# Sliding-window attention block: a new slot table for a block's small tasks, and the norm factors ahead in their slots

## The chip, the cores and the metric

One NeuronCore of a Trainium2 chip runs the whole kernel. The metric is the device time of one execution in microseconds. TensorE is PE in the profile, VectorE is DVE, ScalarE is ACT, GpSimd is POOL, and SyncE, whose queue issues the transfers spoken of here, is SP.

## The reference, cut to what matters

One layer of the trunk is computed: RMSNorm, a sliding-window grouped-query attention with sinks and a SiLU gate, the residual and a final RMSNorm, on 4096 rows of 1024 columns.

```python
xn = rms_norm(x, norm_g[0])
q, k, v, z = jnp.split(xn @ w_in, [1024, 1280, 1536], axis=-1)     # 16 heads, 4 k/v heads of 64
o = banded_attention(q_heads(q), kv_heads(k), kv_heads(v), t5_table, 128, sinks)
y = (merge_heads(o) * jax.nn.silu(z)) @ w_out
return rms_norm(x + y, final_g)
```

## The kernel before, in words

The rows are worked in 16 blocks (`tb`) of 256 rows, each as two tiles of 128. A number is held as a high and a low half in 16 bits, and a product of two such numbers is three passes on PE. The three large projections (q, z and the output o) multiply their operands as 2 x 2 blocks by a scheme of seven products with sums of blocks (`11`, `s1`, `s2`, `12`, `s3`, `s4`, `22` on the left, `11`, `t1`, `t2`, `21`, `t3`, `22`, `t4` on the right) in place of eight plain ones; the first two or three blocks still use the plain form, since the summed weights are only made then. A product of q or z (`product_t`, L324) is 48 matmuls, one of o (`product_o`, L610) 12. The weights of z and o come from DRAM again for each block, 1 MB for a product, by `load_s` (L303) into the tile `ws` of three buffers; in the trace the sources are named wzss, wzs, wost and wos, and wqs for the seventh of q.

A block's work is cut into small tasks, and a table (`STEADY`) gives each task a slot. A slot is about one product on PE; 25 slots make a block, and a block's tasks spread over 62 slots, so that two to three blocks are under way at once. Slots named here count from 0 to 24 within a block's stretch: slot 36 of a table is slot 11 of the next block's stretch. Within a slot the tasks are emitted by phase, in the order bank (copying a finished product out of its bank), attn, sum, split, soft, load, main (the product) and scores. Up to slot 104 a scheduler orders the engines' work; from slot 105 on (block 4, from about 425 us) PE, DVE, ACT and POOL keep exactly the order of emission, and each engine waits in place for what its next instruction needs.

The tasks that matter below:

- `x_square`, `x_factor`, `x_row`, `x_scale`, `x_split` prepare the next block's x. ACT squares (L238), DVE and POOL make the factor 1/rms of each row in `power` (ms L242, rr L244), PE turns two columns of factors into a row (`x_row`, L257, in slot 13), DVE multiplies.
- `out_square`, `out_factor`, `out_store` are the final norm of a tile of 128 output rows: ACT squares (L630), `power` again, DVE multiplies (L637) and SP stores (L639).
- `load_r` (L587) loads the residual of the next output into the one tile `r`, which also holds the output until it is stored. So its transfer waits in SP's queue until the second store has landed, and what stands behind it in the queue waits too.
- A `Pair` (two groups of heads by one tile of rows) goes through scores (L491), post (DVE, L509 and L518), exps (ACT, L526), normalise (DVE, ACT), turn (transposes on PE, L545; pt and pm, L547 to L551), values (L569) and gate (L576). The tile `c` of a pair has two buffers for four pairs a block.
- `proj_k` (L343), `proj_v` (L393), `evac_k` (L377 to L387), `done_q` (L371, L372).

Of the kernel before, what the change touches and what calls it, by code (L numbers as in the profile page):

```python
# [58 lines left out]
def tile_swa_block(ctx, tc, x, xt, t5, norm_g, final_g, w_q, w_kv, w_z, sinks, w_out, hot, out):  # L59
# [589 lines left out]
    def at(phase, s, f, *a):  # L649
        work_of[s][phase].append(lambda: f(*a))  # L650
# [53 lines left out]
    def plain_t(slots, tb, key, names, left, place, done):  # L704
# [8 lines left out]
        "o": (43, 44, 46, 48, 49, 47, 52),  # L713
        "qplain": (0, 1, 2, 3, 4, 5, 6, 6), "zplain": (11, 13, 14, 15, 16, 17, 20, 20),
        "oplain": (43, 44, 46, 47, 48, 49, 50, 50),
# [6 lines left out]

        "pairs": {(0, 0): (10, 11, 14, 15, 20, 13, 14, 16, 20, 22, 25, 28),
# [6 lines left out]
    }  # L730
    SHORT = (0, 1, 2, 3, 5, 2, 3, 4, 5, 7, 8, 9)

    def moved(pairs, by):
# [3 lines left out]
                 zplain=(11, 12, 13, 14, 15, 16, 17, 17), xload=8, pairs=moved(STEADY["pairs"], (7, 5, 4, 2)))  # L737
    LAST = dict(STEADY, vd=13, dv=15, zs12=18, zp22=19, zs22=20,
                pairs={p: tuple(s + d for d in SHORT) for p, s in zip(STEADY["pairs"], (11, 14, 17, 20))},
                o=(31, 32, 33, 35, 36, 34, 37), op=(34, 35, 35, 37), on=(37, 38), om=(37, 38), os=(38, 39), res=32,  # L740
                ysum={"s1": 30, "s2": 31, "s4": 32, "s3": 33},
                ysplit={"11": 29, "s1": 30, "12": 31, "s2": 31, "s4": 32, "s3": 34, "22": 34})

# [2 lines left out]
    def block(tb):  # L746
# [3 lines left out]
        def there(v):  # L750
            if isinstance(v, dict):
                return {k: there(a) for k, a in v.items()}
            return tuple(s0 + s for s in v) if isinstance(v, tuple) else s0 + v

        S = {k: there(v) for k, v in plan.items()}
# [60 lines left out]
        at("load", S["res"], load_r, tb)  # L816
        for t in range(2):
            at("soft", S["on"][t], out_square, tb, t)
            at("soft", S["om"][t], out_factor, tb, t)
            at("split", S["os"][t], out_store, tb, t)  # L820
        if tb + 1 < NTB:
            at("load", S["xload"], load_xin, tb + 1)
            at("load", S["xload"], load_xf, tb + 1)
            for t in range(2):
                at("soft", S["xq"][t], x_square, tb + 1, t)
            at("soft", S["xm"], x_factor, tb + 1)
            at("attn", S["xr"], x_row, tb + 1)
            for i in range(2):
                at("split", S["xscale"][i], x_scale, tb + 1, i)
                at("split", S["xsplit"][i], x_split, tb + 1, i)  # L830
            if tb + 1 >= min(PLAIN["q"], PLAIN["z"]):
                for n in SUM:
                    at("sum", S["xsum"][n], x_sum, tb + 1, n)
                    at("split", S["xsumsplit"][n], x_sum_split, tb + 1, n)

    for tb in range(NTB):
        block(tb)
# [84 lines left out]
```

## Time and profile before

| | us |
|---|---|
| median of three runs | 1491.39 (1479.51 to 1492.14) |
| the profiled execution, its own time | 1487.63 |
| its span, first to last instruction | 1485.9 |
| PE busy | 1371.5 (92%) |
| DVE busy | 1147.8 (77%) |
| ACT busy | 877.5 (59%) |
| POOL busy | 409.3 (28%) |

The span and what lies around it (1.7 us) make the profiled execution's own time. PE is the busiest engine; the other 114 us are the stretches in which no matmul runs. The mean granted TensorE clock is 0.979 of full speed.

### The profile page before, as it was taken

The numbers are of one execution on the slowest core, as the hardware profiler recorded it, in microseconds if no ns is written. First come the engines' busy times: TensorE is split into PE (matmuls) and PEld (weight loads), VectorE is DVE, ScalarE is ACT, GpSimd is POOL, SyncE is SP. The second block draws the span as 40 slices with busy tenths as digits, with TensorE's granted clock in tenths as the row PEclk, the third lists the DMA queues.
The fourth block names the chain that finished last, engine by engine and source line by source line (L and its number), as shares of the span: only waits on it lengthen the run. The fifth ranks groups of instructions, "written<-read, shape, count | busy, mean of one in ns | idle before, by whom it ended". The sixth has DMA issues, their size and how long they took to land.

```text
span 1485.9 us, 39435 instructions
## 1 busy us (share of the span) xinstructions
PE 1371.5 (92%) x16234; PEld 1097.1 (74%) x16234; DVE 1147.8 (77%) x2847; ACT 877.5 (59%) x2313; POOL 409.3 (28%) x402
## 2 busy tenths in 40 slices
PE   5998998998989999898998989999998999999986
PEld 4897687686776878777686777878777686877842
DVE  7489867689577877787777878787787788788883
ACT  8467756576455656565565655556565565656662
POOL 1003422344223231331313223141322323232133
PEclk9999999999999999999999999999999999999998
DMA  9975765968866483765738567493855748374665
GB/s 369 274 274 171 279 244 188 344 245 319 309 230 256 155 322 138 277 232 194 303 103 313 196 218 276 146 354 116 301 210 215 258 165 325 141 266 181 215 239 227
DMA packets 70660, 356.22 MB, mean 240 GB/s; under 512 B 8752, under 2 KB 10832, under 8 KB 40656
## 3 DMA queue, kind: packets, MB, share of 16 engines
q1 hardware_dynamic: 61952, 336.92, 62.2%
q10 hardware_dynamic: 8528, 16.78, 3.0%
q8 instruction: 127, 2.08, 0.6%
q14 instruction: 53, 0.43, 0.1%
HBM read 318.03 MB, written 35.65 MB: 238 GB/s over the span
## 4 chain that ended last, share of the span: by engine, by line
PE 52%; DVE 18%; DMA 17%; ACT 9%; issue 3%; POOL 1%; SPq 1%; ACTq 0%; POOLq 0%; DVEq 0%
PE pa L324 12%; PE pb L324 10%; PE pc L610 8%; DMA ws<-wzss 5%; PE pa L610 4%; PE o L569 4%; PE s L491 3%; DVE q L372 3%; PE pc L324 3%; DMA out<-r 3%; PE pb L610 3%; DVE pm L551 2%; PE tp L545 2%; DVE pt L548 2%; DVE wsp L136 2%
## 5 line engine op out<-in xcount | busy, mean ns | idle before, releaser
L324 PEld LDWEIGHTS <-ws 128*128 128x128 f16 x6192 | 368.1, 101 | 40.8 <-DMA ws<-wzss 21.4
L324 PEld LDWEIGHTS <-wq 128*128 128x128 f16 x4800 | 274.1, 98 | 21.6 <-issue 14.8
L610 PEld LDWEIGHTS <-yo 128*128 128x128 f16 x1380 | 133.8, 99 | 162.9 <-issue 15.8
L526 ACT ACTIVATE c<-c,m 128x129 f32<-128x129 f32 x512 | 198.8, 392 | 21.9 <-DVE m L518 21.5
L610 PE MATMUL pc<-ws,yo 128*128 128x512 f16 x768 | 181.1, 386 | 6.1 <-DMA ws<-wost 3.2
L518 DVE CUSTOM_DVE_ANT_0 c<-s,bias,sink 128x128 f32<-128x128 f32 x496 | 153.6, 348 | 38.3 <-PE tp L545 31.5
L535 ACT ACTIVATE c<-c,rl 128x128 f32<-128x128 f32 x256 | 86.5, 394 | 149.3 <-DVE rl L531 146.1
L244 POOL TENSOR_TENSOR rr<-ms,mhalf 128x1 f32<-128x1 f32 x64 | 35.8, 566 | 416.5 <-DVE ms L242 372.0
L548 DVE SCALAR_TENSOR_TENSOR pt<-tp,pt 128x512 f16<-128x512 f32 x128 | 87.7, 688 | 47.9 <-ACT pt L547 46.7
L491 PE MATMUL s<-K,q 128*128 128x192 f16 x1024 | 109.7, 247 | 12.1 <-DVE m L518 9.6
L597 POOL TENSOR_TENSOR y<-y,y 128x512 f32<-128x512 f32 x52 | 78.3, 1506 | 142.0 <-DVE y L576 80.9
L324 PE MATMUL pb<-xs,ws 128*128 128x128 f16 x1872 | 111.1, 219 | 4.3 <-DMA ws<-wzss 2.4
L537 DVE TENSOR_SCALAR c<-c,rl 128x128 f32<-128x128 f32 x256 | 109.0, 467 | 4.0
L625 POOL TENSOR_TENSOR r<-r,mc 128x512 f32<-128x512 f32 x52 | 74.8, 1443 | 127.2 <-ACT mc L353 73.0
L491 PEld LDWEIGHTS <-q 128*128 128x128 f16 x1024 | 84.9, 98 | 28.8 <-DVE m L518 13.4
L353 ACT ACTIVATE mc<-pa 128x512 f32<-128x512 f32 x68 | 40.5, 595 | 110.7 <-PE pa L324 100.4
L161 POOL TENSOR_TENSOR wst<-wst 128x512 f32<-128x512 f32 x48 | 67.0, 1406 | 111.1 <-ACT wst L196 39.1
L526 ACT ACTIVATION_READ_ACCUMULATOR c<-c,m 128x1 f32 x512 | 96.8, 189 | 0.0
L551 DVE TENSOR_TENSOR pm<-pt,own_m 128x1024 f16<-128x1024 f16 x128 | 92.3, 723 | 3.5
L509 DVE COPY_PREDICATED s<-sel,s 128x128 f32<-128x128 int32 x256 | 72.8, 289 | 25.9 <-PE s L491 25.5
L547 ACT ACTIVATE pt<-tp 128x512 f16<-128x512 f32 x128 | 72.7, 593 | 32.4 <-PE tp L545 28.6
L610 PE MATMUL pa<-ws,yo 128*128 128x512 f16 x384 | 88.3, 379 | 3.5 <-ACT yo L603 1.3
(124 smaller groups left out, 2688.0 us busy)
## 6 DMA issues: line engine op xcount, KB each, us to landing
ws<-wos SPq DMA_DIRECT2D x63, 1024.0 KB, 6.1
ws<-wzss SPq DMA_DIRECT2D x52, 1024.0 KB, 5.9
ws<-wost SPq DMA_DIRECT2D x52, 1024.0 KB, 5.6
ws<-wzs SPq DMA_DIRECT2D x47, 1024.0 KB, 5.2
xin<-in_x SPq DMA_DIRECT2D x32, 512.0 KB, 7.3
xf<-in_xt SPq DMA_DIRECT2D x32, 512.0 KB, 3.9
r<-in_x SPq DMA_DIRECT2D x32, 512.0 KB, 4.3
out<-r SPq DMA_DIRECT2D x32, 512.0 KB, 4.4
```

The lines of the kernel that those rows point to most:

```text
L324: nc.tensor.matmul(place(p, c), left(kc, wi)[:, c * P:(c + 1) * P], right_x(tb, right, kc, xi), start=fresh and c == 0 and k == 0, stop=c ...
L491: nc.tensor.matmul(s[:, hp, 0:3 * HD], lhs, rhs, start=hl == 0, stop=hl == 1)
L509: nc.vector.copy_predicated(dst, sel[:, None, :].to_broadcast([P, 2, HD]), src)
L518: nc.vector.tensor_tensor_reduce(out=cu, in0=sv, in1=b, scale=-1.0 / SCORE, scalar=sink[:, g, r, hp:hp + 1], op0=OP.add, op1=OP.min, accum ...
L526: nc.scalar.activation(cu, cu, AF.Exp, bias=self.m[:, u:u + 1], scale=-1.0, accum_out=self.l[:, u:u + 1])
L535: nc.scalar.activation(cu, cu, AF.Copy, scale=rl[:, u:u + 1])
L537: nc.vector.tensor_scalar(cu, cu, rl[:, u:u + 1], None, op0=OP.mult)
L548: nc.vector.scalar_tensor_tensor(w[:, 1], p, SP, w[:, 0], op0=OP.mult, op1=OP.subtract)
L551: nc.vector.tensor_tensor(self.pm[e].rearrange("p l (h q) -> p (l h) q", h=4), w.rearrange("p l (h q) -> p (l h) q", h=4), own_m[:, None, ...
L597: nc.gpsimd.tensor_tensor(Y[(tb, *dst)], Y[(tb, *l)], Y[(tb, *r)], op=op)
L610: nc.tensor.matmul(p, YO[left][:, yi, c * P:(c + 1) * P], right(c, wi), start=fresh and k == 0, stop=k == 11, skip_group_check=not fresh)
L625: nc.gpsimd.tensor_tensor(r, r, m, op=OP.add)
```

## The change

Two phases change: `out_factor` and `x_factor` go from soft to attn, so that they are emitted ahead of the sum, split and soft tasks of their slot, behind the attn tasks that were registered earlier. And some 45 numbers of the slot table change. None of the products of q, k, v, z and o moves, and no instruction is added or taken away.

```diff
-        "qp22": 10, "qs11": 8, "qs12": 8, "qs22": 13, "vd": 15, "dv": 17,
-        "zp22": 20, "zs11": 18, "zs12": 26, "zs22": 22,
-        "op": (49, 48, 47, 56), "on": (50, 57), "om": (54, 59), "os": (56, 61), "res": 40,
+        "qp22": 9, "qs11": 7, "qs12": 6, "qs22": 15, "vd": 14, "dv": 18,
+        "zp22": 20, "zs11": 18, "zs12": 29, "zs22": 26,
+        "op": (50, 48, 49, 55), "on": (52, 56), "om": (54, 58), "os": (58, 61), "res": 40,
...
-        "pairs": {(0, 0): (10, 11, 14, 15, 20, 13, 14, 16, 20, 22, 25, 28),
+        "pairs": {(0, 0): (10, 11, 14, 20, 22, 12, 13, 17, 18, 20, 25, 27),
...
-        "xload": 5, "xq": (11, 11), "xm": 12, "xr": 13, "xscale": (14, 16), "xsplit": (15, 19),
+        "xload": 5, "xq": (11, 11), "xm": 12, "xr": 13, "xscale": (14, 14), "xsplit": (16, 19),
...
-            at("soft", S["om"][t], out_factor, tb, t)
+            at("attn", S["om"][t], out_factor, tb, t)
...
-            at("soft", S["xm"], x_factor, tb + 1)
+            at("attn", S["xm"], x_factor, tb + 1)
```

A pair's twelve numbers are the slots of scores, post, exps, normalise and turn of its first group, the same five of its second, then values and gate.

On PE, in slots 12 and 13 of a block that is emitted by hand, this stood before (L393 is the last matmul of `proj_v`, L257 is `x_row`, L324 the product `s1` of z):

```order
L393 LDWEIGHTS xb
L393 MATMUL pc<-wkv,xb 128x256
L257 MATMUL tp<-ident,rr 128x128 x2
L324 LDWEIGHTS ws
L324 MATMUL pa<-xs,ws 128x128
```

and this stands now:

```order
L491 LDWEIGHTS q
L491 MATMUL s<-K,q 128x192
L257 MATMUL tp<-ident,rr 128x128 x2
L324 LDWEIGHTS ws
L324 MATMUL pa<-xs,ws 128x128
```

The second scores of the first pair (eight matmuls, L491) have moved from behind product `s1` to ahead of `x_row`.

On DVE, slots 6 to 9, from the gate of a pair (L576) to the copy with which `evac_k` begins (L377), before:

```order
L576 SCALAR_TENSOR_TENSOR y_19519<-o,z 128x512
L637 SCALAR_TENSOR_TENSOR r<-r,rr,gf 128x1024
L548 SCALAR_TENSOR_TENSOR pt_19583<-tp,pt_19583 128x512
L551 TENSOR_TENSOR pm_19586<-pt_19583,own_m 128x1024
L548 SCALAR_TENSOR_TENSOR pt_19593<-tp,pt_19593 128x512
L551 TENSOR_TENSOR pm_19596<-pt_19593,own_m 128x1024
L372 SCALAR_TENSOR_TENSOR q<-cc,q 64x512 x4
L377 COPY K<-K 128x8x128
```

and now:

```order
L576 SCALAR_TENSOR_TENSOR y_19520<-o,z 128x512
L372 SCALAR_TENSOR_TENSOR q<-cc,q 64x512 x2
L548 SCALAR_TENSOR_TENSOR pt_19585<-tp,pt_19585 128x512
L551 TENSOR_TENSOR pm_19588<-pt_19585,own_m 128x1024
L372 SCALAR_TENSOR_TENSOR q<-cc,q 64x512 x2
L242 TENSOR_SCALAR ms<-ss 128x1
L548 SCALAR_TENSOR_TENSOR pt_19631<-tp,pt_19631 128x512
L551 TENSOR_TENSOR pm_19634<-pt_19631,own_m 128x1024
L637 SCALAR_TENSOR_TENSOR r<-r,rr,gf 128x1024
L377 COPY K<-K 128x8x128
```

The first store's multiplication (L637) has gone from ahead of the two turns to behind them, the splits of q (L372) from behind them to ahead and between, and the factor of the second store (L242), which stood behind `evac_k`, is ahead of it. From L377 to the factor of x (`ms<-rs`, L242, right behind the two turns of slot 12) the rows of DVE are otherwise the same in both kernels.

On SP, from the loads of the next x (L105) to the weights of `s4` of z, this stands now:

```order
L105 DMA xf<-in_xt 128x1024 x2
L639 DMA out<-r 128x1024
L303 DMA ws<-wzss_96 128x4096
L303 DMA ws<-wzs_93 128x4096
L99 DMA xin<-in_x 128x1024 x2
L639 DMA out<-r 128x1024
L587 DMA r<-in_x 128x1024 x2
L303 DMA ws<-wzss_92 128x4096
```

Nothing has moved there: the kernel before has the same transfers in the same order.

## Rows read from the trace of the kernel before

**Rows 1.** The page's first part, busy time of each engine, share of the span and instructions; then two stretches of the span, the scheduled part with block 4's beginning and the part in the order of emission, with the busy time of each engine, PE's granted clock, the share of the DMA engines and GB/s.

```profile
PE 1371.5 (92%) x16234; PEld 1097.1 (74%) x16234; DVE 1147.8 (77%) x2847; ACT 877.5 (59%) x2313; POOL 409.3 (28%) x402
...
0.00:425.00 425.00, 380.62 (x4652) 311.38 (x4652) 326.42 (x809) 269.91 (x648) 113.20 (x112) 0.98 0.75 270
425.00:1440.00 1015.00, 961.69 (x11456) 773.99 (x11458) 801.59 (x2010) 593.95 (x1641) 282.04 (x277) 0.98 0.63 228
```

**Rows 2.** The timeline of PE around slots 12 to 16 of block 12, and of the same place in block 7 (last row): start us, us, engine, line, operation, out<-in, form, count, idle before and who ended it.

```profile
1133.63 0.32 PE L257 MATMUL tp<-ident,rr 128*128 128x128 f32 x1 [2.42 <-POOL rr L244]
...
1134.30 2.84 PE L324 MATMUL pa<-xs,ws 128*128 128x128 f16 x48
1136.98 0.82 PE L491 MATMUL s<-K,q 128*128 128x192 f16 x8
...
1147.44 2.85 PE L324 MATMUL pa<-xb,ws 128*128 128x128 f16 x48 [2.75 <-DMA ws<-wzss]
...
708.16 4.48 PE L324 MATMUL pa<-xb,ws 128*128 128x128 f16 x48 [3.68 <-DMA ws<-wzss]
```

**Rows 3.** Seven stretches of 3 us, each right behind `x_row` of one block (7 to 12, and 6 first), columns as in rows 1; PE's granted clock stands behind the busy times.

```profile
606.80:609.80 3.00, 3.00 (x27) 2.94 (x28) 2.25 (x3) 0.00 (x0) 1.77 (x2) 0.50 0.88 315
694.00:697.00 3.00, 3.00 (x52) 2.99 (x53) 2.20 (x2) 0.02 (x1) 1.72 (x2) 1.00 0.87 337
784.30:787.30 3.00, 2.91 (x25) 2.62 (x25) 2.58 (x3) 0.00 (x0) 2.09 (x3) 0.50 0.93 351
873.00:876.00 3.00, 2.86 (x25) 2.63 (x25) 2.57 (x3) 0.00 (x0) 2.08 (x3) 0.50 0.89 335
961.80:964.80 3.00, 3.00 (x31) 3.00 (x29) 1.37 (x2) 0.00 (x0) 0.85 (x1) 0.50 0.59 240
1047.10:1050.10 3.00, 2.83 (x26) 2.67 (x26) 2.53 (x3) 0.00 (x0) 2.04 (x3) 0.50 0.90 333
1134.40:1137.40 3.00, 3.00 (x55) 3.00 (x54) 2.03 (x2) 0.22 (x1) 1.51 (x2) 1.00 0.81 315
```

**Rows 4.** The timeline ahead of `x_row` in block 9, all engines, columns as in rows 2.

```profile
868.68 1.08 ACT L547 ACTIVATE pt<-tp 128x512 f16<-128x512 f32 x2
...
869.30 0.69 DVE L548 SCALAR_TENSOR_TENSOR pt<-tp,pt 128x512 f16<-128x512 f32 x1 [0.43 <-ACT pt L547]
...
871.97 0.21 DVE L242 TENSOR_SCALAR ms<-rs 128x1 f32<-128x1 f32 x2
...
872.20 1.06 POOL L244 TENSOR_TENSOR rr<-ms,mhalf 128x1 f32<-128x1 f32 x2 [8.81 <-DVE ms L242]
```

**Rows 5.** SP's queue: the issue of the second store of each block (every other L639 row is left out), one row for a block.

```profile
602.58 0.38 SPq L639 DMA_DIRECT2D out<-r  x1
...
690.21 0.38 SPq L639 DMA_DIRECT2D out<-r  x1
...
780.41 0.38 SPq L639 DMA_DIRECT2D out<-r  x1
...
869.09 0.38 SPq L639 DMA_DIRECT2D out<-r  x1
...
956.67 0.40 SPq L639 DMA_DIRECT2D out<-r  x1
...
1043.15 0.39 SPq L639 DMA_DIRECT2D out<-r  x1
...
1129.93 0.38 SPq L639 DMA_DIRECT2D out<-r  x1
...
1218.71 0.39 SPq L639 DMA_DIRECT2D out<-r  x1
```

**Rows 6.** SP's queue around the second store of block 12 (its own row is in rows 5), the waits of that queue between 640 and 1240 us (who waited for whom, us in total, times, longest), and the queue at the next-to-last block, where no load of x stands ahead of the store.

```profile
1129.02 0.81 SPq L99 DMA_DIRECT2D xin<-in_x  x2
...
1138.82 0.80 SPq L587 DMA_DIRECT2D r<-in_x  x2
1139.68 2.69 SPq L303 DMA_DIRECT2D ws<-wzss  x2
...
SPq L587 <- DMA out<-r: 57.8, 7, 8.9
...
1306.02 0.34 SPq L639 DMA_DIRECT2D out<-r  x1
1310.29 0.81 SPq L587 DMA_DIRECT2D r<-in_x  x2
```

**Rows 7.** DVE's timeline in slots 7 to 11 of block 9: the first turn's pt, the four splits of q, the copy that begins `evac_k`, the second store's multiplication.

```profile
851.80 0.69 DVE L548 SCALAR_TENSOR_TENSOR pt<-tp,pt 128x512 f16<-128x512 f32 x1 [1.38 <-ACT pt L547]
...
854.58 2.81 DVE L372 SCALAR_TENSOR_TENSOR q<-cc,q 64x512 f16<-64x512 f32 x4
857.40 0.43 DVE L377 COPY K<-K 128x1024 f16<-128x1024 f16 x1
...
867.59 1.28 DVE L637 SCALAR_TENSOR_TENSOR r<-r,rr,gf 128x1024 f32<-128x1024 f32 x1
```

**Rows 8.** One row of the list of waits over the whole span: who waited for whom, us in total, times, longest.

```profile
DVE c L518 <- PE tp L545: 31.5, 11, 2.9
```

**Rows 9.** DVE's timeline at the kernel's end, the last two stores' multiplications.

```profile
1478.43 1.27 DVE L637 SCALAR_TENSOR_TENSOR r<-r,rr,gf 128x1024 f32<-128x1024 f32 x1
...
1480.59 1.28 DVE L637 SCALAR_TENSOR_TENSOR r<-r,rr,gf 128x1024 f32<-128x1024 f32 x1 [0.66 <-POOL rr L244]
```

More of the change, by code (lines that the diff above doesn't have):

```diff
@@ L739, in tile_swa_block @@
                 pairs={p: tuple(s + d for d in SHORT) for p, s in zip(STEADY["pairs"], (11, 14, 17, 20))},
-                o=(31, 32, 33, 35, 36, 34, 37), op=(34, 35, 35, 37), on=(37, 38), om=(37, 38), os=(38, 39), res=32,
+                o=(31, 32, 33, 35, 36, 34, 37), op=(34, 35, 35, 37), on=(37, 38), om=(38, 39), os=(38, 39), res=32,
                 ysum={"s1": 30, "s2": 31, "s4": 32, "s3": 33},
```

12 rows, old and new, of the table STEADY are left out of this document.

## The prediction

> **What bounds the kernel now.** I read the shares first: PE is busy for 92% of the span [rows 1], so the only time to be won is the 114 us in which it does nothing, and what a slow clock costs. Of these, 44 us lie in the first 425 us and 53 us in the 1015 us after it [rows 1]; that second part is eleven blocks of nearly the same course, so a place that costs 1 us there costs 11. Next I read PE's timeline in one of these blocks [rows 2]. It stops in two places. Ahead of `x_row` (L257) it waits 2.42 us for the factor of x, which POOL makes. Ahead of product `s4` of z it waits 2.75 us for its weights. The same two waits stand in other blocks, the second up to 3.68 us long [rows 2].
>
> Each has a follower. Behind the first wait the granted clock is 0.50, the 1.2 GHz level, in five of seven blocks, and PE gets through 25 to 31 matmuls in 3 us where it does 52 to 55 at full clock [rows 3]: some 1.4 us lost. In the block where the second wait was longest, `s4` itself took 4.48 us in place of 2.85 [rows 2]: 1.6 us.
>
> The second wait is the end of a chain on SP. The second store of an output tile is issued at 1129.93 [rows 5] right behind 1 MB of x; the load of `r` waits until that store has landed, 8.9 us later, and the weights of `s4` stand behind it in the queue, at 1139.68 [rows 6]. In seven blocks `r` waited 57.8 us for such stores [rows 6]. `s4` starts at 1147.44, 17.5 us after the store's issue; without the wait it would have started at 1144.69, 14.8 us after.
>
> From one second store to the next the seven blocks took 87.6, 90.2, 88.7, 87.6, 86.5, 86.8 and 88.8 us [rows 5], 88.0 on average. The five in which the clock fell behind `x_row` average 87.4; the one with neither fall took 88.8; the one with the fall at `s4`, 90.2. So a block that lost 1.4 us to the clock behind `x_row` was not slower than one that didn't: the chain of transfers had it wait anyway.
>
> **The change part by part.** *The factor of x.* It goes ahead of the soft tasks in slot 12, but the two turns of that slot were registered earlier in the same phase, and there is no sum or split task on DVE between. So its place on DVE stays: ACT pt twice, DVE pt, pm, pt, pm, then ms, then POOL rr [rows 4]. By itself: 0.
>
> *The second scores of the first pair.* They go from behind `s1` to ahead of `x_row`, into PE's first wait. Their row is 0.82 us, overlapping its neighbours [rows 2]; I take 0.7. The wait becomes 2.42 - 0.7 = 1.7 us, since ms and rr come no earlier. That is the one direct gain: 0.7 us a block. Their data are there: post of the first half ends ahead of the store on DVE, at 867.59 in block 9 [rows 7].
>
> *What is late next.* The second store's place on DVE, its SP row and the loads behind it are as before, so `s4`'s weights come 17.5 us after the store's issue as they do now, while PE is ready after 14.8 - 0.7 = 14.1 us. The wait for them becomes 3.4 us. In a block that is bound like this the 0.7 us are given back whole. Where the shorter first wait no longer makes the clock fall, PE reaches `s4` another 1.4 us earlier and waits for that too.
>
> *Slots 6 to 9.* The first store's multiplication goes behind the turns, the splits of q ahead. DVE has a wait of 1.38 us for pt before, then four pt and pm and four splits, 5.6 us, up to 857.40 [rows 7]. Now two splits fill the wait, and two splits, a factor (0.1 [rows 4]), four pt and pm and the 1.28 us of the store stand in the same stretch: 6 x 0.7 + 0.1 + 1.28 = 5.6 us. `evac_k` begins at the same time, and so does all that follows on DVE to `x_row`. The first store's transfer now starts some 7 us later, beside the weights of `s2`; these are asked for four slots ahead of their product, some 11 us, so 0 on the path.
>
> *The turn of the second pair ahead of the fourth pair's post.* DVE waited 2.9 us in a block for PE to release tile `c` [rows 8]; the order now has the turn first. That wait goes, but DVE is busy for 77% only [rows 1] and PE didn't wait behind it: 0, and it would be paid for only by a DVE that is late.
>
> *The other slots* (exps, normalise, splits of x, sums of y) move by one or two, with at least a slot, some 2.8 us [rows 2], left between each result and the product that reads it: 0. If one were late, it would show as a wait of under 1 us on PE once a block, 11 us in all.
>
> *The end.* The factor of the first of the last two tiles now comes behind the last addition from PE. In the rows, ms to multiplication takes 0.8 us (multiplication at 1478.43 done 1479.70, the next at 1480.59 [rows 9]): its store moves by about that and pushes the second: +0.8 us.
>
> *The scheduled part.* Its rows are rearranged by a scheduler, and no row tells by how much PE's 44 us of waiting [rows 1] change. A good part of them is the start, which the change leaves. I take 0, and 8 us either way for the range, a fifth of it.
>
> **The sum.** Of the ten blocks 4 to 13 I expect four with the clock falling behind `x_row` as now (87.4), three with neither fall (88.8) and three in which it falls at `s4` (90.2): (4 x 87.4 + 3 x 88.8 + 3 x 90.2) / 10 = 88.7 against 88.0, so +7 us. Block 14, whose store lands in 4.3 us [rows 6] and whose chain doesn't bind, gains 0.7. With the end: 1487.6 + 7 - 0.7 + 0.8 = 1494.7, say **1495 us**. The sum is made against the profiled execution's own 1487.63; the median of the three runs, 1491.39, is 3.8 above it, and 1% (15 us) is about what a measurement of this kernel tells from no change.
>
> **The rivals.** *Slower: the clock falls at `s4` in every block.* The mechanism is the one of the block at 690.21: a wait for `s4` that is long enough drops the clock behind it. It decides from a wait somewhere between 2.75 us (no fall) and 3.68 us (fall) [rows 2]; I expect 3.4 us, in between. All ten blocks at 90.2 give +22: 1487.6 + 22 = 1510 us. Against it: a first wait of 1.7 us may still make the clock fall in some blocks, which covers the second.
> The Trainium skill ("TensorE: Matmul & The Clock Gate", section "Why this matters for your kernels") has short pauses of TensorE cost no clock and only longer ones, longer than the one ahead of `x_row`, lower it; by that rule every block would go this way. The trace doesn't agree for the first half: the clock fell behind 2.42 us in five of seven blocks [rows 3].
>
> *Faster: the chain gives way.* If the second store lands earlier than 8.9 us after its issue, as it does in the next-to-last block, with no x ahead of it, in 4.3 us [rows 6], the wait for `s4` goes and the shorter first wait counts in full. Nothing in SP's order moves x away from the store, so this needs luck with the other transfers. Ten blocks at the best seen, 86.5, less 0.7, are 10 x (85.8 - 88.0) = -22: 1465 us.
>
> *The change doesn't do what it says.* The factor of x stays where it is, and all else hides: 1488 us. It speaks for it that the seven blocks' mean, 88.0, is already the chain's.
>
> **How the numbers follow.** Forecast (given back, a little more lost, 1490 to 1503): 0.48. Clock falls everywhere: 0.22. No change, 1488: 0.17. Faster: 0.13. With the scheduled part's 8 us either way the range is 1477 to 1512; what is left out is most of the faster case and the slower one's upper end. Faster by over 1% (below 1476): 0.13 and a little from the scheduled part, 0.14. Slower by over 1% (above 1506): 0.27. Within: 0.59.
>
> **What would show it.** In the changed profile PE's wait ahead of L257 should be 1.7 us in place of 2.42, with eight L491 matmuls ahead of it; the wait for wzss ahead of `s4` should be over 3 us in most blocks; `r` should still wait some 8 us for its store; DVE's wait for PE at L518 should be gone. The forecast is wrong if `s4` starts under 16 us after the second store's issue, if another wait of PE stands in every block, or if the first 425 us differ by more than 8 us.

## The result, and the profile after

The kernel after takes 1497.26 us (median of 14 runs, 1493.45 to 1505.46); the kernel before, run beside it, 1481.05 (14 runs, 1476.42 to 1492.14). The ratio is 1.0104, 95% interval 1.0078 to 1.0130: 12 to 19 us slower. The predicted 1495 us is 2 us off, but the difference forecast was 7 us and the measured one is 16, on the bound of the 1% that the prediction took for no change: the profiled execution on which the sum was made, 1487.63 us, lay 6.6 above the median of before as later runs gave it. That the predicted time was met is luck: a base 6.6 us too high and a difference 9 us too small nearly cancel. An execution that took over 1.5% more than the fastest of its kernel (one each of four kernels below) is left out of medians and ratios, and so is the profile of after_ract_xr14, which is of such a one.

Busy times hardly moved. The first part of the page of the kernel after, and the two stretches that answer to [rows 1] (columns as there):

```profile
PE 1366.1 (91%) x16234; PEld 1095.0 (73%) x16234; DVE 1162.2 (78%) x2847; ACT 874.1 (59%) x2313; POOL 395.1 (26%) x402
...
0.00:425.00 425.00, 371.73 (x4547) 306.91 (x4548) 318.81 (x786) 261.41 (x632) 112.42 (x112) 0.96 0.74 265
425.00:1440.00 1015.00, 957.81 (x11505) 771.77 (x11503) 813.91 (x1998) 592.65 (x1633) 263.98 (x274) 0.99 0.63 228
```

In the first 425 us PE did 105 matmuls fewer than before: the scheduled part is behind. So the span is best cut at `x_row`, which each block has once; the one of block 4 is in slot 113, so the first part so cut holds the scheduled slots and the first eight in the order of emission (`proj_k` of slots 107 and 108 ends at 410.7 us in before, ahead of the 425 us given above for slot 105). PE's timeline at the first matmul of `x_row` of block 4 and of block 14, first before, then after:

```profile
427.82 0.32 PE L257 MATMUL tp<-ident,rr 128*128 128x128 f32 x1 [3.03 <-POOL rr L244]
...
1309.91 0.99 PE L257 MATMUL tp<-ident,rr 128*128 128x128 f32 x2 [2.43 <-POOL rr L244]
```

```profile
438.50 0.32 PE L257 MATMUL tp<-ident,rr 128*128 128x128 f32 x1 [2.37 <-POOL rr L244]
...
1321.91 0.32 PE L257 MATMUL tp<-ident,rr 128*128 128x128 f32 x1 [2.37 <-POOL rr L244]
```

`x_row` of block 4 comes 10.7 us later, the ten blocks from there take 883.4 us in place of 882.1, and the end (to the span's) 172.3 in place of 176.0. Ahead of that PE stops in two places, here in the kernel after and then at the same places before:

```profile
135.64 0.64 PE L569 MATMUL o<-pt,v 128*64 128x512 f16 x2 [6.04 <-ACT pt L547]
...
234.88 1.44 PE L491 MATMUL s<-K,q 128*128 128x192 f16 x8 [5.34 <-ACT K L386]
```

```profile
130.34 0.66 PE L257 MATMUL tp<-ident,rr 128*128 128x128 f32 x2 [5.07 <-DVE pt L548]
...
225.56 0.82 PE L491 MATMUL s<-K,q 128*128 128x192 f16 x8 [1.05 <-ACT K L386]
```

The first stop is hardly new: the kernel before waits 5.07 us there, for pt on DVE. The second is 4.3 us longer, and ACT's timeline shows what held it up:

```profile
233.06 1.15 ACT L196 ACTIVATE wst<-wst,gs 128x1024 f32<-128x1024 f32 x1 [3.04 <-DMA wst<-in_wz]
234.24 1.21 ACT L386 ACTIVATE K<-pb 64x512 f16<-64x512 f32 x2
```

The scheduler has put a multiplication of weights (L196), for whose load ACT waits 3.04 us, ahead of the copy of K (L386) that the scores need; in before L386 stands ahead of it. Of the six kernels here with the new blocks 0 to 3 (one or two numbers aside) five show this order; the sixth, after_ract, waits 3.07 us for the same copy without it, so it is not the head's whole loss.

The 10.7 us are those of one execution. Half of them are there at `x_row` of block 1 already (136.21 us in place of 130.34), where the five others of these kernels have it at 130.1 to 132.1; their `x_row` of block 4 comes at 430.3 to 435.8, 2 to 8 us later than before.

Now the blocks. PE's timeline in block 12 (first three rows, against [rows 2]) and the waits of PE between block 4 and block 14 (who waited for whom, us in total, times, longest):

```profile
1140.45 0.82 PE L491 MATMUL s<-K,q 128*128 128x192 f16 x8
1143.65 0.32 PE L257 MATMUL tp<-ident,rr 128*128 128x128 f32 x1 [2.37 <-POOL rr L244]
...
1156.38 1.86 PE L324 MATMUL pa<-xb,ws 128*128 128x128 f16 x19 [2.33 <-DMA ws<-wzss]
```

```profile
PE tp L257 <- POOL rr L244: 28.1, 20, 2.6
PE pa L324 <- DMA ws<-wzss: 14.9, 7, 3.1
PE tp L545 <- DVE c L537: 3.7, 6, 0.7
```

The eight scores stand ahead of `x_row`, and yet it waits 2.37 us, as long as before. Waits for the weights of `s4` come to 15 us, as before. New is the last row: a turn (L545) that waits for DVE's normalise (L537), 0.5 to 0.7 us in six of the blocks; before, no turn waited there.

Why `x_row`'s wait didn't shrink, DVE's and POOL's timeline in block 9 shows, at the place of [rows 7]:

```profile
861.21 0.56 POOL L244 TENSOR_TENSOR rr<-ms,mhalf 128x1 f32<-128x1 f32 x1 [12.15 <-DVE ms L242]
861.73 1.27 POOL L363 TENSOR_TENSOR cc<-mc 128x512 f32<-128x512 f32 x1
861.85 1.70 DVE L551 TENSOR_TENSOR pm<-pt,own_m 128x1024 f16<-128x1024 f16 x1
...
864.67 0.41 DVE L377 COPY K<-K 128x1024 f16<-128x1024 f16 x1
```

The second store's ms now comes ahead of the last pt and pm; it sets off POOL's rr, and behind rr POOL's sum of a product of q (L363). This runs beside DVE's pm (L551), which takes 1.70 us in place of 0.69. `evac_k` begins 1.6 us after the end of `proj_k`, before 0.7 (medians of ten blocks), and all of DVE up to `x_row`'s factor with it. The Trainium skill ("GPSIMD Engine Reference", section "Key points") says that POOL shares its SBUF interfaces with DVE and gets in the way of instructions with two SBUF inputs; pm has two, and 0.69 against 1.70 us agrees.

The chain on SP, block 12, against [rows 6]:

```profile
1139.04 0.81 SPq L99 DMA_DIRECT2D xin<-in_x  x2
1139.94 0.38 SPq L639 DMA_DIRECT2D out<-r  x1
1147.50 0.80 SPq L587 DMA_DIRECT2D r<-in_x  x2
1148.36 3.37 SPq L303 DMA_DIRECT2D ws<-wzss  x2
```

From the store's issue to `s4` 16.4 us pass, where the prediction carried 17.5 over: the store is issued 0.9 us later against PE, and lands 7.6 us after its issue in place of 8.9.

Last, the clock in four stretches (columns as in [rows 3]): behind `x_row` of blocks 5, 8 and 9 (rows 1, 3, 4), and at `s4` of block 5 (row 2):

```profile
526.50:529.50 3.00, 3.00 (x51) 2.88 (x53) 2.93 (x12) 0.03 (x1) 1.26 (x2) 1.00 0.64 258
539.20:542.20 3.00, 3.00 (x31) 3.00 (x30) 0.21 (x1) 0.42 (x3) 1.26 (x1) 0.50 0.94 391
793.50:796.50 3.00, 2.92 (x49) 2.82 (x49) 2.93 (x13) 0.00 (x0) 1.41 (x3) 1.00 0.76 307
880.50:883.50 3.00, 2.92 (x26) 2.87 (x27) 2.93 (x13) 0.00 (x0) 1.40 (x3) 0.50 0.71 287
```

Behind nearly the same wait (2.37 us, once 2.65) the clock fell in three of the ten blocks and stayed up in seven; in two of these it fell at `s4`.

### The profile page after: what moved, and what is told of

Its sections match the earlier page's. It is cut to its first block, busy times and chain, and to the rows that moved or that the text cites. A ratio compares the mean times of both kernels' runs of the same rounds, so it can differ in the third digit from the quotient of the medians.

```text
span 1494.2 us, 39467 instructions
## 1 busy us (share of the span) xinstructions
PE 1366.1 (91%) x16234; PEld 1095.0 (73%) x16234; DVE 1162.2 (78%) x2847; ACT 874.1 (59%) x2313; POOL 395.1 (26%) x402
## 4 chain that ended last, share of the span: by engine, by line
PE 38%; DVE 26%; DMA 15%; ACT 13%; issue 6%; POOL 1%; SPq 0%; POOLq 0%; ACTq 0%; DVEq 0%
PE pa L324 10%; PE pb L324 7%; PE pc L610 5%; DMA ws<-wzss 4%; DVE pm L551 4%; PE o L569 3%; DVE q L372 3%; PE pc L324 3%; DVE pt L548 3%; PE pa L610 3%; PE pb L610 2%; PE s L491 2%; DMA ws<-wost 2%; ACT xin L238 2%; DVE wsp L136 2%
## 5 line engine op out<-in xcount | busy, mean ns | idle before, releaser
L324 PEld LDWEIGHTS <-ws 128*128 128x128 f16 x6192 | 364.4, 100 | 41.3 <-issue 21.7
L324 PEld LDWEIGHTS <-wq 128*128 128x128 f16 x4800 | 274.8, 98 | 23.2 <-issue 12.2
L491 PE MATMUL s<-K,q 128*128 128x192 f16 x1024 | 109.5, 248 | 16.4 <-ACT K L386 7.5
L604 DVE TENSOR_TENSOR yo<-y,yo 128x512 f16<-128x512 f32 x103 | 72.7, 707 | 50.8 <-ACT yo L603 50.6
L324 PE MATMUL pb<-xs,ws 128*128 128x128 f16 x1872 | 111.0, 219 | 1.0 <-DMA ws<-wzs 1.0
L551 DVE TENSOR_TENSOR pm<-pt,own_m 128x1024 f16<-128x1024 f16 x128 | 108.9, 853 | 3.5
L491 PEld LDWEIGHTS <-q 128*128 128x128 f16 x1024 | 85.7, 98 | 33.8 <-issue 14.2
L282 POOL TENSOR_TENSOR xf<-xf 128x512 f32<-128x512 f32 x56 | 75.9, 1365 | 116.3 <-DVE xb L270 91.0
L537 DVE TENSOR_SCALAR c<-c,rl 128x128 f32<-128x128 f32 x256 | 101.8, 439 | 3.7
L597 POOL TENSOR_TENSOR y<-y,y 128x512 f32<-128x512 f32 x52 | 68.7, 1321 | 106.0 <-DVE yo L604 53.6
L625 POOL TENSOR_TENSOR r<-r,mc 128x512 f32<-128x512 f32 x52 | 70.0, 1349 | 78.0 <-ACT c L526 48.9
```

Of the source, the lines that this page charges most:

```text
L282: nc.gpsimd.tensor_tensor(dst, l, r, op=OP.subtract)
L324: nc.tensor.matmul(place(p, c), left(kc, wi)[:, c * P:(c + 1) * P], right_x(tb, right, kc, xi), start=fresh and c == 0 and k == 0, stop=c ...
L491: nc.tensor.matmul(s[:, hp, 0:3 * HD], lhs, rhs, start=hl == 0, stop=hl == 1)
L537: nc.vector.tensor_scalar(cu, cu, rl[:, u:u + 1], None, op0=OP.mult)
L551: nc.vector.tensor_tensor(self.pm[e].rearrange("p l (h q) -> p (l h) q", h=4), w.rearrange("p l (h q) -> p (l h) q", h=4), own_m[:, None, ...
L604: nc.vector.tensor_tensor(YO[name][:, 1], s, YO[name][:, 0], op=OP.subtract)
```

## The experiments

Each kernel was timed beside before (1481 to 1483 us). The last three columns are read from PE's timeline as above: the time of `x_row` of block 4, from there to that of block 14, and the rest of the span. They are those of one execution of each kernel, which can lie some us from the median (before 6.6 above it, before_ract_xr14 5.3 above, after_no15 3.6 below), so a few us between two rows of them tell little; the medians and intervals decide.

| kernel | median, us | ratio to before (95%) | block 4 | ten blocks | rest |
|---|---|---|---|---|---|
| before | 1481.05 | 1 | 427.8 | 882.1 | 176.0 |
| after | 1497.26 | 1.0104 (1.0078 to 1.0130) | 438.5 | 883.4 | 172.3 |
| old_head | 1494.62 | 1.0086 (1.0055 to 1.0118) | 428.0 | 884.4 | 180.3 |
| new_head | 1493.34 | 1.0078 (1.0050 to 1.0106) | 435.8 | 879.5 | 176.1 |
| before_phase | 1487.36 | 1.0018 (0.9989 to 1.0047) | 430.1 | 879.4 | 176.1 |
| after_qp10 | 1497.44 | 1.0110 (1.0084 to 1.0136) | 432.5 | 886.8 | 177.6 |
| after_om59 | 1497.42 | 1.0108 (1.0080 to 1.0136) | 430.3 | 887.2 | 176.9 |
| before_ract | 1478.07 | 0.9960 (0.9935 to 0.9984) | 427.7 | 874.4 | 177.6 |
| after_ract | 1503.29 | 1.0142 (1.0117 to 1.0167) | 435.1 | 886.4 | 178.2 |
| before_ract_xr14 | 1456.93 | 0.9817 (0.9785 to 0.9849) | 434.5 | 856.7 | 169.3 |
| after_no15 | 1485.11 | 1.0013 (0.9981 to 1.0046) | 424.6 | 879.4 | 175.5 |
| after_no15_blocks | 1494.80 | 1.0090 (1.0055 to 1.0125) | 434.7 | 880.3 | 175.0 |
| after_ract_xr14 | 1460.65 | 0.9841 (0.9792 to 0.9889) | | | |
| old_head_ract_xr14 | 1458.85 | 0.9852 (0.9810 to 0.9895) | 434.6 | 848.6 | 171.3 |

**The two halves of the program.** old_head keeps the old table and phases in blocks 0 to 3; new_head has the new ones there and the old ones from block 4 on.

```diff
-        plan = {0: FIRST, NTB - 2: NEXT_TO_LAST, NTB - 1: LAST}.get(tb, STEADY)
+        plan = {0: FIRST, NTB - 2: NEXT_TO_LAST, NTB - 1: LAST}.get(tb, STEADY if tb >= 4 else OLD)
```

> The old table and the old phases in blocks 0 to 3, the new ones from block 4 on: PE's order is that of the kernel before up to about slot 100, and that of the changed kernel behind it. First theory: the loss lies in the scheduled part, whose x_row of block 4 came at 427.8 us before and at 438.5 after; then this kernel takes 1481 to 1487 us and its block-4 x_row comes at 427 to 430 us. Rival: the loss lies in the blocks in the order of emission; then it takes 1494 to 1500 us.

> The new table and phases in blocks 0 to 3, the old ones from block 4 on. First theory (the loss lies in the scheduled part): 1491 to 1497 us, x_row of block 4 at 436 to 440 us. Rival (it lies in the later blocks): 1481 to 1486 us.

Neither half alone carries the loss: 13 us with the new blocks, 12 with the new head, and 16 with both. The new head is where the table above puts it, 435.8 against 427.8; of old_head's 13 us its profile shows 2 in the ten blocks and 4 at the end against that of before, which lies 6.6 us above its own median.

**The phases alone, on the kernel before.**

```diff
-            at("soft", S["om"][t], out_factor, tb, t)
+            at("attn", S["om"][t], out_factor, tb, t)
...
-            at("soft", S["xm"], x_factor, tb + 1)
+            at("attn", S["xm"], x_factor, tb + 1)
```

In the last block out_factor also goes a slot later, as in the change.

> The kernel before with the phase change alone: out_factor and x_factor in attn (in the last block out_factor a slot later where it needs it), the slot table as it was. Theory (the factors don't move by it to speak of): 1479 to 1486 us, within 0.3% of the kernel before. Rival (the phases make the loss): 1490 us or more.

The median, 1487.4 us, is 1.4 above what the theory gave and 2.6 under the rival. The interval holds no change and ends at 7 us, so most of the 16 us is in the table.

**The late evac_k.** First the sum of q a slot later, then the second store's factor a slot later.

```diff
-        "qp22": 9, "qs11": 7, "qs12": 6, "qs22": 15, "vd": 14, "dv": 18,
+        "qp22": 10, "qs11": 7, "qs12": 6, "qs22": 15, "vd": 14, "dv": 18,
```

> The changed kernel with one number undone: POOL's sum for the last quarter of q (L363) back in slot 10. In the changed kernel it runs beside DVE's pm (L551) in slot 8, which took 1.70 us there in place of 0.69, and evac_k and all behind it came 0.8 us later against PE. Theory: pm is back at 0.69, the wait ahead of x_row goes from 2.37 to some 1.7 us as was predicted, but the wait for the weights of s4 grows by as much: 1494 to 1499 us. Rival (the late DVE sets the block's time): 0.7 us a block, 1487 to 1490 us.

POOL's queue holds the sum right behind rr in either slot, so pm still took 1.70 us and nothing changed: the time is in the theory's range, but the edit didn't do what it was for and tests neither. The next one did:

```diff
-        "op": (50, 48, 49, 55), "on": (52, 56), "om": (54, 58), "os": (58, 61), "res": 40,
+        "op": (50, 48, 49, 55), "on": (52, 56), "om": (54, 59), "os": (58, 61), "res": 40,
```

> The kernel after, with the factor of the second output tile a slot later (slot 59 in place of 58). Its ms then comes on DVE behind evac_k instead of ahead of the last pt and pm, so POOL's rr and the sum of the second product of q (L363) come later too. Theory (POOL beside DVE): pm at L551 takes 0.69 us again in place of 1.70, evac_k's copy of K starts 0.7 us after the end of proj_k in place of 1.6, the second store is issued 0.9 us earlier against PE, and ten blocks get back 9 us: about 1488 us, against 1497 for the kernel after. PE's wait ahead of x_row should fall from 2.37 to about 1.5 us. Rival (the late evac_k is only a symptom; the blocks lose by their other new slots): the time stays at 1495 to 1499 us, whether pm is short again or not.

The timeline of DVE, POOL and PE in block 9 of this kernel, and PE's waits from block 4 on:

```profile
857.43 0.69 DVE L551 TENSOR_TENSOR pm<-pt,own_m 128x1024 f16<-128x1024 f16 x1
...
863.82 1.27 POOL L363 TENSOR_TENSOR cc<-mc 128x512 f32<-128x512 f32 x1
...
874.63 0.32 PE L257 MATMUL tp<-ident,rr 128*128 128x128 f32 x1 [1.65 <-POOL rr L244]
```

```profile
PE pa L324 <- DMA ws<-wzss: 24.4, 10, 3.8
PE tp L257 <- POOL rr L244: 19.5, 20, 2.4
```

POOL's sum now runs behind pm, pm is short again, and `x_row` waits 1.65 us. But the waits for the weights of `s4` rise from 15 to 24 us, and the time is the same to 0.2 us. My theory fell: the late `evac_k` costs nothing clear of noise. What `x_row` saves, `s4` waits; an earlier store does not bring the weights sooner: r is issued 8.3 us after the store in place of 7.6, and `s4` starts 17.0 us after it in place of 16.0 (means of ten blocks). It fits that the 1 MB of weights and the 1 MB of x ahead of the store in the queue are issued where they were against PE; no run here moved them.

**The chain of transfers.** r is loaded from ACT's queue, four slots later; in the third kernel `x_row` also goes a slot later.

```diff
-            nc.sync.dma_start(R[tb, t], x[r0:r0 + P, :])
+            (nc.sync if tb == NTB - 1 else nc.scalar).dma_start(R[tb, t], x[r0:r0 + P, :])
...
-        "op": (49, 48, 47, 56), "on": (50, 57), "om": (54, 59), "os": (56, 61), "res": 40,
+        "op": (49, 48, 47, 56), "on": (50, 57), "om": (54, 59), "os": (56, 61), "res": 44,
...
-        "xload": 5, "xq": (11, 11), "xm": 12, "xr": 13, "xscale": (14, 16), "xsplit": (15, 19),
+        "xload": 5, "xq": (11, 11), "xm": 12, "xr": 14, "xscale": (14, 16), "xsplit": (15, 19),
```

> The kernel before, with the loads of r (L587) issued from ACT's queue, four slots later, in all blocks but the last; the loads of s4's weights on SP no longer stand behind a load that waits for the second store. Theory (the chain store, r, weights of s4 holds PE back in the blocks 4 to 13): PE's waits for wzss there, 15.5 us in all, go, and with them what the slow clock costs behind the longest: 15 to 25 us less than before, 1457 to 1467 us. Rival (the chain is hidden anyway, the waits of PE only move to x_row or to the scores): within 5 us of before, 1477 to 1487 us.

> The same edit on the kernel after. Theory (the ten blocks of the kernel after lose because their second store, and so the chain behind it, comes 0.9 us later): without the chain the blocks of both kernels take the same time, and only the scheduled first part still differs, by 8 to 10 us: 1466 to 1476 us, 8 to 10 above the kernel before with this edit. Rival (the late evac_k costs PE its 0.9 us a block by x_row, chain or not): 15 to 18 us above the kernel before with this edit.

> The kernel before with the loads of r on ACT's queue, and x_row a slot later (14 in place of 13), behind one more group of scores. Theory (without the chain the waits ahead of x_row, 25.6 us in ten blocks, count in full): they fall under 5 us, and the clock no longer falls behind them; 20 to 30 us less than with the loads of r on ACT's queue alone, 1430 to 1445 us. Rival (the later x_row makes xs late and the wait stands ahead of the first product of the next block): no gain against the loads of r alone.

PE's waits from block 4 on in before_ract, after_ract and before_ract_xr14, in this order:

```profile
PE tp L257 <- POOL rr L244: 27.1, 20, 3.0
PE pa L610 <- DMA ws<-wos: 11.9, 10, 2.1
```

```profile
PE tp L257 <- POOL rr L244: 24.0, 19, 2.6
PE tp L545 <- DVE c L537: 5.7, 9, 0.7
```

```profile
PE pa L610 <- DMA ws<-wos: 8.3, 10, 2.0
```

In before_ract no product of the ten blocks waits for wzss any more, where 15.6 us went before, but weights of o are waited for in every block, 12 us in place of 3; 5 us are gained in place of the 15 to 25 of the theory, and the time is in the rival's range. These weights are issued just behind r, as the queues of SP and ACT in block 10 of before_ract show:

```profile
973.68 0.34 ACTq L587 DMA_DIRECT2D r<-in_x  x1
...
976.06 4.10 SPq L303 DMA_DIRECT2D ws<-wos  x2
```

The Trainium skill ("DMA: Bandwidth & Descriptors", section "Issuing engines are not separate DMA queues") has transfers of all engines run on the same 16 DMA engines and interleave. The trace agrees: a load of wos lands 7.1 us after its issue (median of all) in place of 6.1 before.

after_ract missed both of its expectations: 25 us above before_ract, with the chain gone from both. In the profiles 7 us of this lie ahead of block 4's `x_row` and 12 in the ten blocks. There the turn's wait is 5.7 us, and the clock fell behind `x_row` in nine of the ten blocks and twice more, in before_ract in seven; by the clock's records of the two traces that is 37.5 us at half clock against 23.9, some 6.8 us.

A slot for `x_row` is what pays. Its wait is gone in all ten blocks, the clock fell in one of them, and before_ract_xr14 is 1.8% faster than before, with the lowest median of the study. It is 21 us faster than before_ract, as expected (20 to 30); the 1430 to 1445 us were built on a before_ract that didn't come. The later `x_row` without r on ACT's queue was not run.

**One number.** In the change the normalise of the first half of the first pair went from slot 15 to 20, its turn from 20 to 22. The number is put back in all blocks, then from block 4 on alone.

```diff
-        "pairs": {(0, 0): (10, 11, 14, 20, 22, 12, 13, 17, 18, 20, 25, 27),
+        "pairs": {(0, 0): (10, 11, 14, 15, 22, 12, 13, 17, 18, 20, 25, 27),
```

> The kernel after, with one number of the table put back: the normalise of the first half of a block's first pair in slot 15 in place of 20, its turn still in slot 22. Theory (the ten blocks lose by the turn that PE starts 0.3 to 0.7 us before DVE's normalise is done): these waits, 3.7 us in ten blocks of the kernel after and 5.6 with r on ACT's queue, go, and nothing else changes: 1491 to 1494 us against 1497. Rival (the chain of transfers takes the gain back as it did that of the short pm): the waits go and the time stays at 1496 to 1499 us.

> The kernel after, with the normalise of the first half of the first pair back in slot 15 in the blocks 4 to 14 alone; the first four blocks keep slot 20, so PE's order there is that of the kernel after. Putting it back in all blocks gave 12 us. Theory (the traces of that pair: some 4 us by the turn's wait in the ten blocks, the rest in the scheduled first part): 1492 to 1494 us. Rival (the ten blocks lose the 12 us, and the difference of the first parts, 424.6 against 438.5 us, is what one execution differs from another): 1484 to 1487 us. Rival (it is all in the first part): 1496 to 1499 us.

Why a turn two slots behind its normalise waits: DVE and PE in block 9 of the kernel after, around that turn.

```profile
907.19 0.68 DVE L548 SCALAR_TENSOR_TENSOR pt<-tp,pt 128x512 f16<-128x512 f32 x1
907.90 1.25 DVE L551 TENSOR_TENSOR pm<-pt,own_m 128x1024 f16<-128x1024 f16 x1
909.08 0.68 DVE L604 TENSOR_TENSOR yo<-y,yo 128x512 f16<-128x512 f32 x1
909.68 0.16 DVE L531 RECIPROCAL rl<-l 128x4 f32<-128x4 f32 x1
909.88 0.48 DVE L537 TENSOR_SCALAR c<-c,rl 128x128 f32<-128x128 f32 x2
...
910.22 0.74 PE L545 MATMUL tp<-ident,c 128*128 128x128 f32 x4 [0.64 <-DVE c L537]
```

The normalise stands behind a pt, a pm and a split of y, 2.5 us of DVE (907.19 to 909.68), and DVE goes from one to the next without a stop; so it ends after PE has come to the turn. With the number put back the row `PE tp L545 <- DVE c L537` all but goes (0.2 us), and the ten blocks take 879.4 us. PE's waits in that kernel from block 4 on, and the timeline of ACT and PE at the second place in the head:

```profile
PE tp L257 <- POOL rr L244: 23.0, 18, 2.4
PE pa L324 <- DMA ws<-wzss: 12.1, 8, 2.8
...
PE tp L545 <- DVE c L537: 0.2, 1, 0.2
```

```profile
224.26 1.21 ACT L386 ACTIVATE K<-pb 64x512 f16<-64x512 f32 x2
...
224.90 0.82 PE L491 MATMUL s<-K,q 128*128 128x192 f16 x8 [2.62 <-ACT K L386]
```

The copy of K (L386) no longer stands behind the multiplication of weights (L196), the scores wait 2.62 us for it, and `x_row` of block 4 comes at 424.6 us, 14 earlier than after and 6 to 11 earlier than in the five other kernels with the new head. With the number put back only from block 4 on, both waits of the head are there again, and so is its time:

```profile
131.52 0.64 PE L569 MATMUL o<-pt,v 128*64 128x512 f16 x2 [6.69 <-ACT pt L547]
...
230.64 1.44 PE L491 MATMUL s<-K,q 128*128 128x192 f16 x8 [5.70 <-ACT K L386]
```

So of the 12 us that the one number costs, some 10 go with the scheduled head: 1494.8 to 1485.1, two kernels that differ in that number in blocks 0 to 3 alone and whose intervals don't meet. The 2 to 3 that go with the blocks (1497.3 to 1494.8) have the size of the turn's wait, but their intervals overlap. Both expectations were missed in size: 1485.1 is 6 us under the theory of after_no15, which had left the head out, and 1494.8 is 0.8 above that of after_no15_blocks; its rival with all in the blocks is out, the one with all in the head is not. Why this number has the scheduler order the head otherwise, and whether another small change would do it too, no run here shows. Without that number the change can't be told from none: 1.0013, from 3 us faster to 7 slower.

**The change on top of the better kernel.**

> The kernel after with both edits, r on ACT's queue and x_row a slot later; in the kernel before they took 26 us off. Theory (what the change costs is the turn's wait, some 5 us in ten blocks, and the first 425 us, 5 to 10 us; the rest of the difference is how often the clock falls behind x_row): without the waits at x_row and s4 the clock stays up in both kernels and the change costs 10 to 15 us: 1467 to 1472 us, against 1457 for the kernel before with both edits. Rival (the change's other places cost a block 1 to 1.5 us of their own, as the pair with r on ACT's queue suggests, 25 us apart): 1475 to 1482 us.

> Both edits on the kernel with the old table and phases in blocks 0 to 3 and the new ones from block 4. Theory (first part and blocks both cost): 5 to 10 us less than the kernel after with both edits, and about 5 us above the kernel before with both, 1460 to 1464 us. Rival (the whole loss is in the first part): level with the kernel before with both edits, 1455 to 1459 us. Rival (the whole loss is in the later blocks): level with the kernel after with both edits.

With both edits of before_ract_xr14 the kernel after takes 1460.7 us, and with the old head 1458.9, against 1456.9. That is 2 to 4 us by the medians and 4 to 5 by the ratios, where I expected 10 to 15; both forecasts of after_ract_xr14 lie above its median. The three intervals overlap: a cost of the change on top of these edits is not shown, and none of the three forecasts of old_head_ract_xr14 is settled.

**What stays open.** The parts don't add up in one case: by the last pair the blocks of the kernel after cost 2 to 3 us, but old_head, which has these blocks and the old head, is 13 slower than before (8 to 17 by its interval). Its clock fell at `s4` in four of the ten blocks, where a fall costs (in before in one), and its end is 4 us longer; whether this is the kernel's or that of one execution no run here tells.

## Why the prediction was right, and where it was wrong

- *The factor of x stays in place, 0.* Right: the rows of DVE ahead of `x_row` are the same, and the phases alone cost nothing clear of noise (1.0018).
- *The second scores take 0.7 us off `x_row`'s wait, and `s4`'s weights take it back.* The mechanism is right, and after_om59 shows both sides of it: 1.65 us where 1.7 was predicted, and 24 us of waits for wzss in place of 15. In the kernel after itself it didn't come about, because of the next step. The sum had it cost 7 us over ten blocks; after_om59, where it came about, takes as long as the kernel after, where it didn't (1497.4 and 1497.3 us). No run shows the 7 us; the intervals of these two leave room for some 6 either way.
- *Slots 6 to 9: 5.6 us, evac_k begins at the same time.* Wrong by 0.9 us: the sum counted DVE's work at its price alone and not what the moved factor sets off on POOL beside it. It cost nothing that the runs show.
- *17.5 us from the second store to `s4` "as they do now".* Wrong as a constant: 17.5 was block 12's, the ten blocks average 17.1 before, 16.0 in the kernel after, whose store goes out 0.9 us later against PE, and 17.0 in after_om59, where it does not. So the weights don't follow the store.
- *The turn ahead of the fourth pair's post: DVE's wait goes, 0.* Right: the row of [rows 8] is no longer in the list.
- *The other slots: 0, with at least a slot between each result and its reader; a late one would show as a wait of under 1 us on PE once a block.* This is the step that failed, and the waits look as it said: 0.5 to 0.7 us at L545. One of the slots was late, since a slot is a place in an order and not a time: 2.5 us of DVE's work stood ahead of that normalise. I had looked at the distance to the reader and not at the row of DVE.
- *The scheduled part: 0, 8 us either way.* Wrong: 10.7 us later at block 4 in the profiled execution, 2 to 8 in five other kernels with this head, and some 10 us of the time by that same number. It is the largest part of the loss. The 8 us were a guess, and the ends of the range, 1477 and 1512, are not the sum of terms shown (1490 - 8 and 1503 + 8 are 1482 and 1511).
- *The end, +0.8 us.* From the last sum to the first store's multiplication 0.61 us passed before (1477.82 to 1478.43), now 1.42 (1485.89 to 1487.31): right.
- *Forecast of the blocks: four with the clock falling behind `x_row`, three with neither fall, three at `s4`.* It was three, five and two; the mean block 88.3 us, not 88.7. The rule of the Trainium skill that was weighed there ("TensorE: Matmul & The Clock Gate", section "Why this matters for your kernels"), by which only a longer pause lowers the clock, didn't hold: it fell behind 2.37 us at `x_row`, and behind 1.92 and 2.33 us at `s4`. Nor did the first rival's bounds at `s4`, no fall at 2.75 us and one at 3.68: these two falls lie under the lower one, and at 3.15 us (block 7) the clock stayed up.

By its own signs the forecast was wrong: `x_row` waited 2.37 us and not 1.7, the wait ahead of `s4` was over 3 us in one block and not in most, `s4` started under 16 us after the store in six of the ten blocks, a new wait of PE stood in six, and the first part ended 10.7 us late. So the time was met by luck, with a sum whose two largest terms were wrong: +7 us in the blocks, where 1 to 5 were lost, and 0 in the head, where some 10 were. The rivals didn't come: no chain gave way, and the clock at `s4` fell in two blocks, not in all.

## What to carry to other kernels

When a table of slots is changed, look for each moved producer at what stands ahead of it in its engine's own row, not only at how many slots lie between it and its reader: here one number of some 45 made 12 of the 16 us, some 10 of them by what a scheduler made of it. Where two waits stand one behind the other in a block and the second is for transfers, shorten both or none; the first alone (1.65 in place of 2.37 us) gave nothing, and r's load alone 5 us of 15. What a scheduler makes of the same numbers is to be read from the order of its rows and not to be put at zero.

## What the runs showed that I had not expected

- A 16-bit multiplication on DVE (128x1024, two inputs) takes 0.69 us alone and 1.70 beside a sum of 1.27 us on POOL, so POOL's work is not free where DVE is bound to an order.
- A wait of 2.37 to 2.43 us ahead of `x_row` was followed by the 1.2 GHz level in some blocks and not in others, from three of ten (after) to nine of ten (after_ract), with the same instructions of PE ahead of it. In after_om59 the clock fell even behind 1.66 us, and at `s4` of block 10 it stayed up behind 3.53 us. Row 2 of this fence is at the `s4` of block 6, row 3 behind the `x_row` that waited 1.66 us, row 1 behind one that waited 1.65 and didn't fall:

```profile
606.00:609.00 3.00, 2.81 (x49) 2.73 (x49) 2.93 (x12) 0.00 (x0) 1.58 (x3) 1.00 0.95 335
619.60:622.60 3.00, 3.00 (x31) 3.00 (x29) 0.00 (x0) 0.00 (x0) 0.98 (x1) 0.50 0.96 404
1230.40:1233.40 3.00, 3.00 (x32) 3.00 (x30) 2.96 (x9) 0.00 (x0) 0.53 (x1) 0.50 0.70 281
```
